# A two-layer encoder trunk on one core: layer-norm sums in one PSUM bank, consecutive dense matmuls on alternating banks, other first transfers and another last output

## The chip, the cores and the metric

The kernel runs on one core of one Trainium2 chip. The metric is the device time of one execution in microseconds (us); of several runs the median is given. A profiled execution also gives a trace: every instruction on the matrix engine (PE, with its weight loads as PEld), the vector engine (DVE), the scalar engine (ACT), GpSimd (POOL) and SyncE (SP), which here only issues transfers, and every DMA transfer. The span of the trace reaches from the first to the last instruction; the profiled execution's own time is a little longer.

## The reference

256 tokens of 2048 numbers pass two layers. Each layer is a mixer, a cross-attention into 256 memory tokens and a gated convolutional FFN, each on an RMS norm of the stream and added to it:

```python
for layer in range(DEPTH):
    h = rms_norm(x, norm_mix_g[layer])
    if layer % 2 == 0:
        # conv branch: GLU, depthwise conv of width 31, LayerNorm, swish; and differential attention
        x = x + mixer_conv_diff(h, ...)
    else:
        x = x + mixer_s5(h, ...)          # state-space scan both ways, GELU, GLU
    x = x + memory_cross_attention(rms_norm(x, norm_xa_g[layer]), rms_norm(mem, norm_mem_g[layer]), ...)
    x = x + conv_ffn(rms_norm(x, norm_ffn_g[layer]), ...)
return rms_norm(x, final_g)
```

Everything is float32. The LayerNorm of the conv branch (`conformer_conv`) is the one whose sums the change touches: mean and variance over 1024 channels, `y = (xf - mu) * lax.rsqrt(var + eps) * g + b`. The last line is the final RMS norm over 2048 numbers of a token.

## The kernel before

**Weights and splitting.** Nearly all the work is dense products of the 256 tokens with weights that come from memory. A weight tile of 128 x 1024 numbers (`raw`, 512 KB, four buffers) is fetched by SP (L204), split by ACT into a rounded high part `hi` (L209) and by DVE into the rest, `lo` (L211); the activations are kept as a high and a low part too. The product is then the sum of three matmuls in a faster format, high by high, low by high and high by low. This is the helper `wtile`, and every dense layer goes through it, 960 times in all.

**Two shapes of product.** `lin_ws` (glu, q and k, memory keys, cross-attention queries, FFN up) holds weights still in the array: a weight block of 128 x 128 against the tokens. For each of 16 input blocks (`kk`) and each of two output blocks (`c`), it issues a short matmul of 256 columns (L253, the weights' low part) and a long one of 512 columns (L250, the weights' high part against both parts of the activations). Output block c accumulates in its own PSUM bank, so the order of banks is 0, 0, 1, 1. One call is 64 matmuls. `lin_xs` (values, output projections, FFN down, the S5's GLU) holds the activations still: for each input block and each half of the tokens (`tb`) three matmuls of 512 columns (L287), with a bank for each half: banks 0, 0, 0, 1, 1, 1.

**Order of the work.** The program is written out by a scheduler with a timing model, which sets the order on each engine. Work beside the dense stream (the depthwise convolution and its LayerNorm `conv_ln`, the S5's parameters) is a Python generator in a list `side`; after each weight tile, `background` lets as much of it into the program as a credit allows. What is left when the memory's keys and values are done is drained, and then the output projection of the first mixer starts with its first half (`bo`, the differential attention's heads) for two output chunks, and its second half (`ao`, the conv branch).

**PSUM buffers.** Besides two `acc` tiles for the dense products there is a pool with two tags, `ps` and `pt`, of two banks each. `pst()` without a tag alternates between the two. The attention heads take two `ps` banks for scores and then `pt` banks for the transposed weights (L457), the output (L463) and its transpose (L476). In `conv_ln` the sums over channels are matmuls with a matrix of ones: `ps_mu` (L518) takes one bank by `pst()`, `ps_var` (L527) the next by another `pst()`.

**First and last.** At the start SP fetches the first quarter of `x`, the identity matrix, gains, the first weight tile and the other quarters in turn with further tiles; POOL fetches five small arrays. At the end the last `lin_xs` keeps the second token half's matmuls of the last three weight tiles for the end (L290, `tail=3`). Then for each half: add to the stream (L694), square and sum (ACT, L696), multiply the last quarter by the final gain (L697; the other quarters had theirs earlier), the reciprocal square root on 128 x 1 numbers (`rsqrt_steps`, L111 to L118: two integer steps and three iterations of four operations), scaling by quarters on ACT (L706) and DVE (L708), and eight output transfers (L709).

## Time and profile before

| | |
|---|---|
| median of 3 runs | 2935.66 us (2931.55 to 2938.13) |
| profiled execution, its own time | 2932.71 us |
| its span | 2930.9 us |
| PE busy, granted clock | 98% of the span, 0.994 |
| DVE, ACT, POOL busy | 76%, 51%, 9% |
| memory traffic | 674 MB, 230 GB/s on average |

A matmul record's end is modelled, and consecutive matmuls overlap in the records: a matmul of 512 columns is recorded with 0.39 us while the next starts 0.23 us after it. So the rate of PE is read from starts, or from the chain of waits, which counts each matmul until the next one starts. The timeline merges neighbours of one line on one engine into one row with a count; the time in brackets is idle time of that engine before the row, and what ended it. Rows named PEld are weight loads and run beside the matmuls.

### The profile page before, as it was taken

How to read it: one execution, taken by the hardware profiler on the slowest of the kernel's cores; microseconds unless marked ns; L12 is line 12 of the kernel's file. 1: busy time of each engine (PE TensorE's matmuls, PEld its weight loads, DVE VectorE, ACT ScalarE, POOL GpSimd, SP SyncE). 2: the span in 40 equal slices, each digit the busy share in tenths (PEclk: the TensorE clock that was granted, in tenths of full speed). 3: DMA queues.
4: the chain of work that ended last, by engine and by line, in shares of the span. 5: the costliest groups of instructions: out<-in, count | busy, mean ns of one | idle time of the engine just before them, and what ended most of it. 6: DMA issues, size and time to landing. Idle time of an engine off the chain costs nothing. (4 is left out here: it accounts for less than half of the span.)

```text
span 2930.9 us, 44468 instructions
## 1 busy us (share of the span) xinstructions
PE 2881.2 (98%) x16769; PEld 2436.5 (83%) x16769; DVE 2213.4 (76%) x3568; ACT 1493.2 (51%) x2015; POOL 268.2 (9%) x509
## 2 busy tenths in 40 slices
PE   8999998999999999999999999999999999999998
PEld 7887887788888888888887787888888888888886
DVE  7899987877899987889855894656567776467764
ACT  5545554554455543455544554545455554345543
POOL 2100022222210012020021121000000000000000
PEclk9999999999999999999999999999999999999999
DMA  6655578988997687776697787655455555555554
GB/s 220 231 188 172 190 238 270 297 260 277 292 297 250 233 272 256 266 254 234 235 316 275 288 328 276 208 187 187 161 191 191 186 188 192 194 189 184 190 188 150
DMA packets 206023, 674.16 MB, mean 230 GB/s; under 512 B 33152, under 2 KB 35728, under 8 KB 205296
## 3 DMA queue, kind: packets, MB, share of 16 engines
q1 hardware_dynamic: 177376, 593.96, 59.1%
q0 software_dynamic: 28432, 77.36, 8.1%
q8 instruction: 131, 2.15, 0.3%
q14 instruction: 84, 0.69, 0.1%
HBM read 620.48 MB, written 61.08 MB: 233 GB/s over the span
## 5 line engine op out<-in xcount | busy, mean ns | idle before, releaser
L211 DVE TENSOR_TENSOR lo<-raw,hi 128x1024 fp32r<-128x1024 f32 x960 | 1173.6, 1224 | 546.1 <-ACT hi L209 542.6
L250 PE MATMUL ps_ws<-x,hi 128*128 128x512 f32 x4352 | 1527.8, 397 | 5.3 <-ACT hi L209 4.4
L209 ACT CAST hi<-raw 128x1024 fp32r<-128x1024 f32 x960 | 1009.0, 1051 | 1005.1 <-PE ps_xs L287 460.8
L253 PE MATMUL ps_ws<-x,lo 128*128 128x256 f32 x4352 | 1202.8, 282 | 2.9 <-DVE lo L211 2.9
L250 PEld LDWEIGHTS ps_ws<-x,hi 128*128 128x128 f32 x4352 | 809.5, 188 | 187.4 <-ACT hi L209 5.2
L253 PEld LDWEIGHTS ps_ws<-x,lo 128*128 128x128 f32 x4352 | 821.6, 189 | 20.0 <-DVE lo L211 5.0
L287 PE MATMUL ps_xs<-hi,hb 128*128 128x512 f32 x1396 | 432.0, 390 | 0.0
L287 PEld LDWEIGHTS ps_xs<-hi,hb 128*128 128x128 f32 x1396 | 262.0, 188 | 53.9
L287 PE MATMUL ps_xs<-lo,hb 128*128 128x512 f32 x698 | 272.3, 390 | 0.0
L287 PE MATMUL ps_xs<-hi,x 128*128 128x512 f32 x640 | 202.8, 395 | 0.2 <-ACT hi L209 0.2
L851 POOL DMA_DIRECT2D w1s<-d_pw x256 | 122.5, 486 | 602.2 <-PE ps_s L438 263.3
L287 PE MATMUL ps_xs<-hi,oT 128*128 128x512 f32 x512 | 160.8, 392 | 0.8 <-ACT hi L209 0.8
L287 PE MATMUL ps_xs<-hi,gT 128*128 128x512 f32 x512 | 159.3, 391 | 0.3 <-ACT hi L209 0.3
L287 PEld LDWEIGHTS ps_xs<-lo,hb 128*128 128x128 f32 x698 | 131.0, 188 | 27.0
L287 PEld LDWEIGHTS ps_xs<-hi,x 128*128 128x128 f32 x640 | 119.9, 189 | 30.3 <-issue 6.1
L287 PE MATMUL ps_xs<-lo,x 128*128 128x512 f32 x320 | 127.3, 398 | 0.0
L259 ACT COPY z<-ps_ws 128x512 f32<-128x512 f32 x88 | 51.7, 587 | 137.6 <-PE ps_ws L250 137.5
L287 PEld LDWEIGHTS ps_xs<-hi,gT 128*128 128x128 f32 x512 | 96.1, 188 | 21.3 <-issue 1.0
L656 ACT ACTIVATE c<-z,fdb,fdw 128x256 f32<-128x256 f32 x176 | 96.2, 595 | 33.0 <-DVE z L651 32.9
L287 PEld LDWEIGHTS ps_xs<-hi,oT 128*128 128x128 f32 x512 | 96.0, 188 | 20.3 <-ACT hi L209 1.0
L512 DVE SCALAR_TENSOR_TENSOR av<-hpt,cdw,av 128x256 f32<-128x256 f32 x240 | 110.7, 485 | 0.7
L260 DVE TENSOR_TENSOR z<-ps_ws,z 128x512 f32<-128x512 f32 x88 | 60.8, 691 | 55.5 <-ACT z L259 55.5
(285 smaller groups left out, 2654.6 us busy)
## 6 DMA issues: line engine op xcount, KB each, us to landing
raw<-ffn_w_up SPq DMA_DIRECT2D x352, 512.0 KB, 3.4
raw<-ffn_w_down SPq DMA_DIRECT2D x176, 512.0 KB, 4.3
raw<-ab_w_in SPq DMA_DIRECT2D x64, 512.0 KB, 3.3
raw<-xa_wv SPq DMA_DIRECT2D x64, 512.0 KB, 3.4
raw<-xa_wk SPq DMA_DIRECT2D x64, 512.0 KB, 4.5
raw<-xa_wq SPq DMA_DIRECT2D x64, 512.0 KB, 4.3
raw<-xa_wo SPq DMA_DIRECT2D x64, 512.0 KB, 3.6
w1s<-d_pw POOLq DMA_DIRECT2D x256, 64.0 KB, 6.1
```

What stands on the lines that cost most here:

```text
L209: nc.scalar.copy(hi, raw)
L211: ins = nc.vector.tensor_tensor(lo, raw, hi.bitcast(F32), op=ALU.subtract)
L250: both = lambda: nc.tensor.matmul(ps[:, c], lhsT=hi[:, kk, sl], rhs=x2, start=first, stop=last)
L253: nc.tensor.matmul(ps[:, c, 1], lhsT=lo[:, kk, sl], rhs=xh, start=False, stop=False)
L259: self.nc.scalar.copy(out, ps[:, :, 1])
L260: self.nc.vector.tensor_tensor(out, ps[:, :, 0], out, op=ALU.add)
L287: ins = mm()
L512: nc.vector.scalar_tensor_tensor(ac[:, ct, :], hp[:, ct, j : j + NTOK], cdw[:, ct, j : j + 1], ac[:, ct, :], op0=ALU.mult, op1=ALU.add)
L656: nc.scalar.activation(c[:, i], zt[:, i, 1 : NTOK + 1], AF.Identity, bias=fdb[:, ft : ft + 1], scale=w(1))
L851: nc.gpsimd.dma_start(pw[t * 16 : t * 16 + 16], self.d_pw[t, k * 4 : k * 4 + 4].partition_broadcast(16))
```

## The change

1. `lin_ws` and `lin_xs` issue the same matmuls in another order. In `lin_ws` the two short ones come one after the other, then the two long ones, so banks alternate 0, 1, 0, 1 (in the first input block the long ones come first). In `lin_xs` the token half is the inner loop.
2. `conv_ln` takes one bank and uses its two halves for the two sums.
3. `rsqrt_steps` multiplies its argument by -0.5 once and joins operations: 9 operations in three iterations in place of 12, and 6 where the tile is one column wide.
4. At the start the identity comes before `x`, the first weight tile is issued from ACT's queue, and the five small arrays come from SP's queue behind the first `lin_ws` in place of POOL's; the small computation of `lam` that needs one of them is written behind the glu stage.
5. At the end the last product's two token halves accumulate in two separate tiles of the pool in place of one `acc` tile; the multiplication by the last quarter's gain is joined with the scaling; quarter 0 and 3 are scaled by DVE, 1 and 2 by ACT.

```diff
@@ setup @@
+        nc.sync.dma_start(self.ident, a["ident"])
         nc.sync.dma_start(self.X[:, :, 0:512], a["x"][0])
-        nc.sync.dma_start(self.ident, a["ident"])
+        self.begun = False
@@ rsqrt_steps @@
+        nc.vector.tensor_scalar(v, v, -0.5, None, op0=ALU.mult)
         for it in range(3):
-            nc.vector.tensor_tensor(t, y, y, op=ALU.mult)
-            nc.vector.tensor_tensor(t, t, v, op=ALU.mult)
-            nc.vector.tensor_scalar(t, t, -0.5, 1.5, op0=ALU.mult, op1=ALU.add)
-            nc.vector.tensor_tensor(out if it == 2 else y, y, t, op=ALU.mult)
+            if v.shape[-1] == 1:
+                nc.vector.scalar_tensor_tensor(t, y, y, v, op0=ALU.mult, op1=ALU.mult)
+            else:
+                nc.vector.tensor_tensor(t, y, y, op=ALU.mult)
+                nc.vector.tensor_tensor(t, t, v, op=ALU.mult)
+            nc.vector.scalar_tensor_tensor(out if it == 2 else y, t, 1.5, y, op0=ALU.add, op1=ALU.mult)
@@ wtile @@
-        dma = nc.sync.dma_start(raw, src)
+        dma = (nc.sync if self.begun else nc.scalar).dma_start(raw, src)
+        self.begun = True
@@ lin_ws @@
-                for c in range(2):
-                    sl = slice(c * 128, c * 128 + 128)
-                    both = lambda: nc.tensor.matmul(ps[:, c], lhsT=hi[:, kk, sl], rhs=x2, start=first, stop=last)
-                    if first:
-                        both()
-                    nc.tensor.matmul(ps[:, c, 1], lhsT=lo[:, kk, sl], rhs=xh, start=False, stop=False)
-                    if not first:
-                        both()
+                sl = [slice(c * 128, c * 128 + 128) for c in range(2)]
+                both = lambda c: nc.tensor.matmul(ps[:, c], lhsT=hi[:, kk, sl[c]], rhs=x2, start=first, stop=last)
+                low = lambda c: nc.tensor.matmul(ps[:, c, 1], lhsT=lo[:, kk, sl[c]], rhs=xh, start=False, stop=False)
+                for part in (both, low) if first else (low, both):
+                    for c in range(2):
+                        part(c)
@@ lin_xs @@
-                for tb in range(2):
-                    sl = slice(tb * 128, tb * 128 + 128)
-                    ops = [(xh, hi, first, False), (xh, lo, False, False), (xl, hi, False, last)]
-                    for x, y, st, sp in ops:
+                for x, y, st, sp in [(xh, hi, first, False), (xh, lo, False, False), (xl, hi, False, last)]:
+                    for tb in range(2):
+                        sl = slice(tb * 128, tb * 128 + 128)
@@ mixer0, behind the first lin_ws @@
+                for t, v in ((cdw, a["conv_dw"]), (cv, a["conv_v"]), (lq, a["diff_l"].partition_broadcast(128)), (nabs, a["nabs"]), (sub_g, a["subln_g"])):
+                    nc.sync.dma_start(t, v)
@@ conv_ln @@
-        pm = self.pst("ps_mu")
+        pm = self.pst("ps_ln")
+        pv = pm[:, NTOK:]
+        pm = pm[:, :NTOK]
...
-        pm = self.pst("ps_var")
         for ct in range(8):
-            nc.tensor.matmul(pm[:, :NTOK], lhsT=self.ones, rhs=sq[:, ct, :], start=ct == 0, stop=ct == 7)
+            nc.tensor.matmul(pv, lhsT=self.ones, rhs=sq[:, ct, :], start=ct == 0, stop=ct == 7)
@@ ffn, the last product @@
-                ps = self.lin_xs(..., tail=3 if last and n == 3 else 0)
+                ps = self.lin_xs(..., ps=[self.pst(f"ps_e{tb}", ("ps", "pt")[tb]) for tb in range(2)] if last and n == 3 else None, start=True, tail=3 if last and n == 3 else 0)
...
-            nc.vector.tensor_tensor(x, x, fg[:, 1536:2048], op=ALU.mult)
...
-                if n % 2:
+                if n == 3:
+                    nc.vector.scalar_tensor_tensor(x, x, r, fg[:, 1536:2048], op0=ALU.mult, op1=ALU.mult)
+                elif n:
                     nc.scalar.activation(x, x, AF.Copy, scale=r)
```

How the order on the engines moves is seen at three places. The first is PE in an FFN-up product of the second layer, within one weight tile; `x2` is the tile of activations, `lo` and `hi` the parts of the weight tile. Before:

```order
L253 MATMUL ps_ws_24100<-x2_20730,lo_24171 128x256
L250 MATMUL ps_ws_24100<-x2_20730,hi_24169 128x512
L253 MATMUL ps_ws_24100<-x2_20730,lo_24171 128x256
L250 MATMUL ps_ws_24100<-x2_20730,hi_24169 128x512
L253 MATMUL ps_ws_24100<-x2_20730,lo_24171 128x256
```

And now, around the end of one product and the start of the next:

```order
L255 MATMUL ps_ws_22684<-x2_20699,lo_22755 128x256 x2
L254 MATMUL ps_ws_22684<-x2_20699,hi_22753 128x512 x2
L254 MATMUL ps_ws_22787<-x2_20189,hi_22790 128x512 x2
L255 MATMUL ps_ws_22787<-x2_20189,lo_22792 128x256 x4
L254 MATMUL ps_ws_22787<-x2_20189,hi_22790 128x512 x2
L255 MATMUL ps_ws_22787<-x2_20189,lo_22792 128x256 x2
```

Short and long matmuls alternated one by one; now they come in pairs, and at a product's start four long and four short ones follow each other.

The second place is PE at the LayerNorm's second sums. `ps_oT` is the transpose of a head's output, `bo` the heads' part of the output projection's input, `sq` the squares. Before:

```order
L287 MATMUL ps_xs_4728<-lo_4762,bo_2510 128x512
L287 MATMUL ps_xs_4728<-hi_4760,bo_2510 128x512
L287 MATMUL ps_xs_4728<-hi_4779,bo_2510 128x512
L476 MATMUL ps_oT_3050<-ident_76,on_3026 128x128 x2
L527 MATMUL ps_var_3960<-sq_3883,ones_81 128x256 x8
L287 MATMUL ps_xs_4728<-lo_4781,bo_2510 128x512
```

And now:

```order
L254 MATMUL ps_ws_4048<-x2_2417,hi_4075 128x512 x2
L527 MATMUL ps_ln_3853<-sq_3863,ones_81 128x256 x8
L255 MATMUL ps_ws_4048<-x2_2440,lo_4100 128x256 x2
L475 MATMUL ps_oT_2898<-ident_76,on_2876 128x128 x2
L456 MATMUL ps_wT_2929<-ident_76,s_2903 128x128 x4
```

The second sums stood behind the last head's transpose, in the middle of the output projection. They now stand in the memory keys' products, ahead of the sixth of eight heads' transpose and 39 dense matmuls behind the first sums.

The third place is DVE at the end: `ps_e0` and `ps_e1` are the last product's two token halves, `fg` the final gains, `fv` and `rsq` the reciprocal square root's small tiles, `fr` its result. Before:

```order
L694 TENSOR_TENSOR X_75<-X_75,ps_xs_26693 128x512 x2
L697 TENSOR_TENSOR X_75<-X_75,fg_26307 128x512
L700 TENSOR_REDUCE fv_26878<-ss_26306 128x1
L697 TENSOR_TENSOR X_75<-X_75,fg_26307 128x512
L700 TENSOR_REDUCE fv_26910<-ss_26306 128x1
L701 TENSOR_SCALAR fv_26878<-fv_26878 128x1
```

And now:

```order
L118 SCALAR_TENSOR_TENSOR rsq_t_26850<-rsq_i_26849,fv_26845 128x1
L122 SCALAR_TENSOR_TENSOR fr_26846<-rsq_t_26850,rsq_i_26849 128x1
L694 TENSOR_TENSOR X_75<-X_75,ps_e1_26661 128x512
L709 TENSOR_SCALAR X_75<-X_75,fr_26846 128x512
L705 SCALAR_TENSOR_TENSOR X_75<-X_75,fr_26846,fg_26274 128x512
L699 TENSOR_REDUCE fv_26871<-ss_26273 128x1
```

Both halves' additions stood first and their small steps alternated; now the first half's chain stands whole ahead of the second half's addition.

More of the change, by code (lines that the diff above doesn't have):

```diff
@@ L261, in add_parts, with lin_xs @@
         return out
-    def lin_xs(self, w, xt, kts, ps=None, stop=True, tail=0):
+    def lin_xs(self, w, xt, kts, ps=None, stop=True, tail=0, start=False):
         nc = self.nc
-        start = ps is None
-        if start:
+        start = start or ps is None
+        if ps is None:
             ps = self.acc.tile([128, 2, 512], F32, tag="acc", name="ps_xs")
@@ L515, in conv_ln @@
         sh = [128, 4, NTOK]
-        pm = self.pst("ps_mu")
+        pm = self.pst("ps_ln")
+        pv = pm[:, NTOK:]
+        pm = pm[:, :NTOK]
         for ct in range(8):
-            nc.tensor.matmul(pm[:, :NTOK], lhsT=self.ones, rhs=ac[:, ct, :], start=ct == 0, stop=ct == 7)
-        nc.vector.tensor_scalar(mu, pm[:, :NTOK], 1.0 / 1024, None, op0=ALU.mult)
+            nc.tensor.matmul(pm, lhsT=self.ones, rhs=ac[:, ct, :], start=ct == 0, stop=ct == 7)
+        nc.vector.tensor_scalar(mu, pm, 1.0 / 1024, None, op0=ALU.mult)
         sq = S.tile([128, 8, NTOK], F32, tag="A0", name="sq")
@@ L672, in ffn @@
                 last = half == 1 and layer == 1
-                ps = self.lin_xs(a[f"ffn_w_down{layer}"][n, k0 : k0 + nk // KD], hv, list(range(nk)), tail=3 if last and n == 3 else 0)
+                ps = self.lin_xs(a[f"ffn_w_down{layer}"][n, k0 : k0 + nk // KD], hv, list(range(nk)), ps=[self.pst(f"ps_e{tb}", ("ps", "pt")[tb]) for tb in range(2)] if last and n == 3 else None, start=True, tail=3 if last and n == 3 else 0)
                 if last and n == 3:
```

23 lines of the change are left out of this document (9 added, 14 removed).

## The prediction

> **What bounds the kernel now.** I read the page first, then the chain of waits, the timeline at the places where PE stands still, and the windows of those stages. PE is recorded busy for 98% of the span, with the two lines of `lin_ws` on top; DVE and ACT have room over the whole.
>
> ```profile
> span 2930.9 us, 44468 instructions
> PE 2881.2 (98%) x16769; PEld 2436.5 (83%) x16769; DVE 2213.4 (76%) x3568; ACT 1493.2 (51%) x2015; POOL 268.2 (9%) x509
> L250 PE MATMUL ps_ws<-x,hi 128*128 128x512 f32 x4352 | 1527.8, 397 | 5.3 <-ACT hi L209 4.4
> L253 PE MATMUL ps_ws<-x,lo 128*128 128x256 f32 x4352 | 1202.8, 282 | 2.9 <-DVE lo L211 2.9
> ```
>
> So the time is the number of matmuls by their rate, and a few stops. The rate stands in the chain of waits (start, length, line, count), where a matmul counts until the next one starts:
>
> ```profile
> 2304.23 0.46 PE ps_ws L250 x2
> 2305.04 0.24 PE ps_ws L253 x2
> 2383.24 0.46 PE ps_ws L250 x2
> ...
> 2451.19 130.56 PE ps_xs L287 x576
> ...
> 2912.20 4.09 PE ps_xs L290 x18
> ```
>
> 576 long matmuls of `lin_xs` take 130.56 us, 226.7 ns each. For `lin_ws`, the row of two long ones marks where one product ends and the next starts; from 2304.23 to 2383.24 seven products pass, 224 pairs of a short and a long one in 79.01 us: 352.7 ns a pair. What short ones cost in a row is seen in the second cross-attention, where 15 of them start between the first and the second of these rows of the timeline (1.80 us, 120.0 ns each):
>
> ```profile
> 2004.12 0.28 PE L574 MATMUL ps_xs<-kT,qT 128*128 128x256 f32 x1
> 2005.92 0.28 PE L253 MATMUL ps_ws<-x,lo 128*128 128x256 f32 x1
> ```
>
> One long and one short one by these rates are 346.7 ns. The alternation in `lin_ws` costs 6.0 ns a pair more.
>
> **The change part by part. Banks in `lin_xs`: nothing.** The 18 late matmuls (L290) all write one bank and take 227.2 ns each; the 576 change the bank at every third one and take 226.7. A same-bank neighbour costs nothing here, and the lines issue the same matmuls, so I put 0.
>
> **Order in `lin_ws`: -10.8 us.** There are 4352 / 2 = 2176 groups of two short and two long ones. At 352.7 ns a pair a group takes 705.4 ns; without any cost of alternation it would be 693.4. The new order changes between lengths once up and once down in a group in place of twice. The rows with x2 show such neighbours as they already stand at a product's edge: two short ones 0.24 us, two long ones 0.46, together 0.70 (rounded to 0.01, so this only says that it lies between the two). I take half the extra as gone, 6.0 ns a group. The bounds: all of it, 12.0 ns; and nothing, since there are stretches in which alternation is free, such as ten pairs between these starts (3.46 us, 346 ns a pair):
>
> ```profile
> 858.12 0.39 PE L250 MATMUL ps_ws<-x,hi 128*128 128x512 f32 x1
> 861.58 0.39 PE L250 MATMUL ps_ws<-x,hi 128*128 128x512 f32 x1
> ```
>
> 2176 groups by 6.0 ns are 13.1 us. Ahead of the first output projection (8 glu, 8 q and k, 8 key products, 24 of 136) DVE is nearly full with the convolution, and I count no gain there:
>
> ```profile
> 200.00:300.00 100.00, 100.00 (x460) 80.77 (x459) 94.92 (x204) 54.59 (x89) 0.00 (x0) 1.00 0.52 178
> ```
>
> (PE, PEld, DVE, ACT, POOL busy, then clock, DMA share and GB/s.) That leaves 112/136 of it, 10.8 us; bounds 0 and 26.
>
> **LayerNorm's bank: -9.6 us.** The largest stop of PE is in the first output projection, for `ao`:
>
> ```profile
> L523 ACT ACTIVATE sq<-av x2: 1056/1059/1062, 403.0 to 404.9; 128x1024 f32<-128x1024 f32 x2
> ...
> 401.26 0.42 DVE L519 TENSOR_SCALAR hpt<-ps_mu 128x256 f32<-128x256 f32 x1
> ...
> 470.87 0.38 PE L476 MATMUL ps_oT<-ident,on 128*128 128x128 f32 x2
> 471.08 3.62 PE L527 MATMUL ps_var<-sq,ones 128*128 128x256 f32 x16
> ...
> 480.93 0.39 PE L287 MATMUL ps_xs<-hi,bo 128*128 128x512 f32 x1
> 491.26 0.79 PE L287 MATMUL ps_xs<-hi,ao 128*128 128x512 f32 x1 [9.94 <-ACT ao L299]
> 494.35 0.39 PE L287 MATMUL ps_xs<-lo,ao 128*128 128x512 f32 x1
> ```
>
> The squares are done at 406, yet their sums start at 471.08, right behind the last head's transposes: the second bank is taken from the buffers that the heads still use. In one bank they follow the squares. From the sums to `ao` took 20.2 us; even if DVE needs twice that between the heads, `ao` is there by 450, 30 us ahead of its use. The stop from 480.93 to 491.26, less one matmul, is 10.1 us. Behind it the clock is half: the seven starts from 491.26 to 494.35 take 3.09 us, at 226.7 ns they would take 1.59. Together 11.6 us. What is late next is the weights:
>
> ```profile
> 440.00:460.00 20.00, 19.95 (x111) 16.81 (x109) 14.99 (x23) 9.09 (x13) 3.81 (x8) 1.00 1.02 324
> 481.00:491.00 10.00, 0.32 (x2) 0.00 (x0) 8.10 (x12) 5.19 (x8) 0.00 (x0) 0.65 0.87 291
> 491.00:510.00 19.00, 18.74 (x81) 15.47 (x82) 13.72 (x17) 9.87 (x16) 3.81 (x8) 0.91 0.49 144
> ...
> ACT hi L209 <- DMA raw<-ab_w_out: 10.0, 6, 3.0
> ```
>
> The transfers are full ahead of the stop and used it to catch up; behind it half is free (0.49 over 19 us, room for the 8.7 us of transfer time that ran in the stop). In this stage (440 to 530) ACT waited 10.0 us for weights, covered so far by four buffers. I take 2 us as showing. Bounds: 0 and 11.6.
>
> **The new wait in it.** PE now meets the second sums 39 dense matmuls, 39 x 0.176 = 6.9 us, behind the first. Mean, subtraction and squares took from 401.3, where DVE reads the first sums, to 406, 4.8 us. Were they later, PE would stand with all dense matmuls behind it, and DVE's `lo` too once its buffers are full; 2 us of room, and I put 0.
>
> **The end: -4.2 us.** After the last matmul the chain of waits and the timeline read:
>
> ```profile
> 2916.32 0.70 DVE X L694
> 2917.04 0.73 ACT junk L696 x2
> 2917.80 0.69 DVE X L697
> 2919.31 0.19 DVE fv L701 x2
> 2921.99 0.08 DVE fr L118
> ...
> 2922.09 2.56 ACT L706 ACTIVATE X<-X,fr 128x512 f32<-128x512 f32 x4 [3.57 <-DVE fr L118]
> 2922.10 1.67 DVE L708 TENSOR_SCALAR X<-X,fr 128x512 f32<-128x512 f32 x4
> 2922.61 4.47 SPq L709 DMA_DIRECT2D out<-X  x8
> ```
>
> Although half 0 is complete at 2912.20, where the 18 late ones begin, its addition waits until 2916.32: the tile is one. In separate tiles half 0 goes: addition 0.70, squares 0.73, then a reduction and ten small steps of about 0.19 each, 2.1 us: `fr` at 2915.8. ACT's two scalings (0.62 each) end at 2917.0, as half 1's addition does. Its squares end at 2917.8; DVE scales half 0 meanwhile (0.42 and, for the joined form, 0.69) until 2918.1; reduction and ten steps to 2920.2; DVE's first quarter at 2920.6, everything scaled at 2921.5. SP needs 0.56 us an issue, so the last of four is out at about 2922.9 in place of 2927.08 (2922.61 + 4.47). What follows, 3.8 us to the end of the span, stays. Bounds: 3 (half 0's chain delays half 1 by a us) and 5.5.
>
> **The start: -2.0 us.**
>
> ```profile
> 10.02 1.04 ACT L209 CAST hi<-raw 128x1024 fp32r<-128x1024 f32 x1 [2.35 <-DMA raw<-ab_w_in]
> 4.50:26.40 21.90, 17.48 (x40) 1.00 0.84 293
> 0.00:10.00 10.00, 1.94 (x8) 1.57 (x8) 0.97 (x2) 3.68 (x7) 6.44 (x18) 1.00 0.74 206
> 10.00:20.00 10.00, 7.91 (x39) 6.83 (x40) 5.68 (x10) 8.69 (x19) 0.00 (x0) 1.00 1.01 396
> ```
>
> The first weights arrive at 10.0; ACT, which splits them and evacuates every transposed `x`, then sets the pace until 26.4 (second row: ACT alone, busy 17.48 of 21.90). Its idle 4.4 us are the upper bound, 0 the lower. The small arrays out of the way, 206 GB/s should come nearer to the later 396, and the first tile in at about 6.5; but ACT's order now has the split first, so that the squares that filled 4.55 to 6.0 wait too. I take 2.0. The Trainium skill (Trainium Kernel Development and Optimization, Key Constraints) says that all queues share the same 16 DMA engines and that another issuing engine saves only issue time; by that, at 206 GB/s, the first tile, `x` and the rest (1.2 MB) would be in at 7.8, and the term -1.
>
> **Small: -0.4 us.** The reciprocal roots lose two of twelve steps; most run beside PE. Ahead of the S5, PE waits 2.3 us for a chain with one of them, two steps of 0.19.
>
> ```profile
> 1563.39 2.82 PE L1024 MATMUL ps_u<-ident,xg 128*128 128x128 f32 x12 [2.31 <-DVE xg L1018]
> ```
>
> Sum: -10.8 - 9.6 - 4.2 - 2.0 - 0.4 = -27.0 us. The profiled execution took 2932.7 us (span 2930.9 and 1.8 around it), so 2905.7. The median shown is 3.0 above that execution: 2908.7, rounded to 2908.
>
> **The rivals.** *The order in `lin_ws` is free* (0.26): the stretch at 858 runs at the summed rate while alternating, so the extra may be a matter of how the stream has locked in, not of the changes. Then 2908 + 10.8 = 2919. [...]
>
> *All of the extra goes* (0.14): 21.6 in place of 10.8 us, 2897. For it: pure rows of either length never show it; against it: one change up and down is left in each group.
>
> *The wait for `ao` becomes one for weights* (0.13): most of the 10.0 us of ACT's waits come to light, 2908 + 8 = 2916. Against: the last 19 us of slack.
>
> *Slower* (0.05): a weight load's record is 188 ns, and two short matmuls in a row leave each next load only 120. If the second short and the first long one waited for their loads, a group would take 2 x 68 ns more, 300 us in all. It decides from 7.4 ns a group on, where the other 16.2 us are used up; beyond 10 ns the kernel is slower. Against: the x2 row of short ones with 0.24, and the 15 in a row.
>
> ```profile
> L287 PEld LDWEIGHTS ps_xs<-hi,hb 128*128 128x128 f32 x1396 | 262.0, 188 | 53.9
> ```
>
> *The change does little of what it says* (0.04): order free and the stop replaced together, 2908 + 10.8 + 9.6 = 2928.
>
> **How the numbers follow.** My forecast, 2908, has 0.38, with 2900 to 2915 as its own range. The range of 8 in 10 reaches to the free order above and to the full gain below: 2894 to 2922. Less than 0.2%, 5.9 us, this kernel's runs can't tell from no change. Forecast, the first three rivals and most of the last are below 2929.8: faster 0.91; same 0.05; slower 0.04.
>
> **What would show it.** In the chain of waits of the changed kernel the distance between two products of the FFN up: 11.29 us now, 11.19 by my forecast, 11.1 with all the extra gone, unchanged if the order is free. The second sums near 408 and no stop at `ao`; a stop for `hi` or `lo` within the output projection would be the third rival. At the end half 0's addition some 4 us ahead of half 1's. Weights' first split at 6 to 7. Wrong would be a `lin_xs` rate other than 226.7, or a group of `lin_ws` above 705 ns.

## The result and the profile after

The changed kernel takes 2915.4 us (median of 4 executions, 2915.1 to 2916.2) against 2934.5 of the kernel before: the ratio is 0.9935, interval 0.9918 to 0.9952. Run once more (five executions, 2910.4 to 2918.7, median 2913.4) the ratio is 0.9936, interval 0.9922 to 0.9949. So it is 19 us faster, and 7 us slower than the forecast of 2908.

The head of the page of the changed kernel, profiled at 2915.3 us:

```profile
span 2913.5 us, 44430 instructions
PE 2869.7 (98%) x16769; PEld 2426.1 (83%) x16769; DVE 2203.7 (76%) x3524; ACT 1492.0 (51%) x2015; POOL 266.0 (9%) x504
```

The span is 17.4 us shorter (2930.9 to 2913.5). To see where, I numbered the 13696 dense matmuls of both traces, which are the same in both kernels, and compared when the same number starts:

| stretch | before | changed | difference |
|---|---|---|---|
| start to matmul 256 | 63.6 us | 59.9 us | -3.7 |
| 256 to 1280 (rest of glu, q and k, values) | 201.5 | 200.7 | -0.8 |
| 1280 to 3072 (heads, LayerNorm, first output projection, queries of the cross-attention) | 431.5 | 432.6 | +1.1 |
| 3072 to the last | 2219.3 | 2209.2 | -10.1 |
| the last one's start to the end | 15.0 | 11.1 | -3.9 |

The third row, "the middle stage" from here on, is where I had expected -9.6.

**The dense order.** The chain of waits of the changed kernel shows four long ones in a row at the edge of two products of the FFN up. Here the first and the last of nine products, and the row of `lin_xs`:

```profile
2238.67 0.93 PE ps_ws L254 x4
...
2339.17 0.93 PE ps_ws L254 x4
...
2440.14 130.57 PE ps_xs L289 x576
```

100.50 us for nine: one product now takes 11.17 us (11.29 before). `lin_xs` with its new order of banks takes 130.57 us for 576 matmuls, where it took 130.56.

That is the second layer, whose 44 FFN-up products take 5.3 us less than before in all. The first layer's 44 gain only 3.0 us, since in the kernel before some of its alternating stretches ran faster. Two starts of short matmuls there, with 27 pairs of a short and a long one between them:

```profile
951.87 0.28 PE L253 MATMUL ps_ws<-x,lo 128*128 128x256 f32 x1
...
961.23 0.27 PE L253 MATMUL ps_ws<-x,lo 128*128 128x256 f32 x1
```

That is 346.7 ns a pair, as much as one short and one long matmul by themselves, and not 352.7. Nine whole products of the kernel before take 11.10 to 11.12 us, less than the 11.17 of the new order; seven of the nine stand right behind a product that was held up (11.9 us or more).

**The LayerNorm.** In PE's timeline of the changed kernel the second sums stand at 396, and the first matmul that reads `ao` comes without a stop:

```profile
396.26 3.62 PE L527 MATMUL ps_ln<-sq,ones 128*128 128x256 f32 x16
...
480.21 0.62 PE L289 MATMUL ps_xs<-hi,ao 128*128 128x512 f32 x2
```

But PE now stands at other places, in the same output projection and in the queries of the cross-attention behind it. Two of them, from the timeline (in brackets the idle time ahead of the row and what ended it):

```profile
503.23 1.04 ACT L301 CAST kT<-kvraw 128x1024 fp32r<-128x1024 f32 x1 [7.17 <-DMA kvraw<-d_kT]
504.18 1.04 ACT L214 CAST hi<-raw 128x1024 fp32r<-128x1024 f32 x1
...
505.27 0.73 PE L289 MATMUL ps_xs<-hi,bo 128*128 128x512 f32 x2 [2.23 <-ACT hi L214]
...
545.56 0.69 DVE L845 TENSOR_TENSOR w1t<-w1s 128x512 f32<-128x512 f32 x1 [4.64 <-DMA w1s<-d_pw]
546.17 1.22 DVE L216 TENSOR_TENSOR lo<-raw,hi 128x1024 fp32r<-128x1024 f32 x1
...
547.45 0.73 PE L289 MATMUL ps_xs<-lo,ao 128*128 128x512 f32 x2 [1.10 <-DVE lo L216]
```

ACT waits 7 us for a tile of the memory's keys, and the weights' split is queued behind it; DVE waits 4.6 us for a piece of the S5's first weights (`w1s`, side work), and the next `lo` is queued behind that. The waits of ACT for weights between 440 and 640, before and then in the changed kernel (us in total, times, longest):

```profile
ACT hi L209 <- DMA raw<-xa_wq: 23.9, 11, 5.2
ACT hi L209 <- DMA raw<-ab_w_out: 12.7, 8, 3.0
```

```profile
ACT hi L214 <- DMA raw<-ab_w_out: 32.7, 19, 6.3
ACT hi L214 <- DMA raw<-xa_wq: 30.8, 12, 4.3
```

And the window 440 to 600 as one row, before and then changed (PE, PEld, DVE, ACT, POOL busy; clock; share of the DMA engines; GB/s):

```profile
440.00:600.00 160.00, 145.16 (x699) 120.29 (x698) 130.40 (x206) 78.10 (x113) 38.23 (x80) 0.95 0.88 284
```

```profile
440.00:600.00 160.00, 151.91 (x749) 124.14 (x747) 124.54 (x187) 73.02 (x101) 42.13 (x88) 0.99 0.93 294
```

PE gets 50 more records into the window, the transfers' share goes from 0.88 to 0.93. PE's own waits between 300 and 640, the largest rows before and then in the changed kernel:

```profile
PE ps_xs L287 <- ACT ao L299: 9.9, 1, 9.9
PE ps_xs L287 <- DVE lo L211: 3.6, 5, 1.5
```

```profile
PE ps_xs L289 <- DVE lo L216: 4.5, 8, 1.1
PE ps_ws L255 <- DVE lo L216: 4.1, 5, 1.6
PE ps_xs L289 <- ACT hi L214: 3.5, 4, 2.2
```

With the smaller rows they add up to 15.0 us before and 14.9 in the changed kernel. The stop at `ao` went, and its 10 us are spread over some twenty smaller ones, nearly all for `hi` and `lo`. (In the second profile of the changed kernel they add up to 10.3.)

**Start and end.** Timeline of the changed kernel: the first split is at 4.73 (10.02 before; forecast at 6 to 7), and at the end the first half's addition is 4.08 us ahead of the second's:

```profile
4.73 1.04 ACT L214 CAST hi<-raw 128x1024 fp32r<-128x1024 f32 x1 [2.27 <-DMA raw<-ab_w_in]
...
2898.79 0.69 DVE L694 TENSOR_TENSOR X<-X,ps_e 128x512 f32<-128x512 f32 x1 [1.77 <-PE ps_e L289]
2902.25 0.16 DVE L122 SCALAR_TENSOR_TENSOR fr<-rsq_t,rsq_i 128x1 f32<-128x1 f32 x1
2902.87 0.69 DVE L694 TENSOR_TENSOR X<-X,ps_e 128x512 f32<-128x512 f32 x1 [0.46 <-PE ps_e L292]
```

### The profile page after: what moved, and what is told of

Its sections match the earlier page's. It is cut to its first block, busy times and chain, and to the rows that moved or that the text cites. A ratio compares the mean times of both kernels' runs of the same rounds, so it can differ in the third digit from the quotient of the medians.

```text
span 2913.5 us, 44430 instructions
## 1 busy us (share of the span) xinstructions
PE 2869.7 (98%) x16769; PEld 2426.1 (83%) x16769; DVE 2203.7 (76%) x3524; ACT 1492.0 (51%) x2015; POOL 266.0 (9%) x504
## 5 line engine op out<-in xcount | busy, mean ns | idle before, releaser
L254 PE MATMUL ps_ws<-x,hi 128*128 128x512 f32 x4352 | 1351.4, 396 | 2.8 <-DVE x L168 1.2
L255 PEld LDWEIGHTS ps_ws<-x,lo 128*128 128x128 f32 x4352 | 793.6, 188 | 186.6 <-DVE lo L216 10.5
L255 PE MATMUL ps_ws<-x,lo 128*128 128x256 f32 x4352 | 844.7, 280 | 6.7 <-DVE lo L216 6.6
L254 PEld LDWEIGHTS ps_ws<-x,hi 128*128 128x128 f32 x4352 | 674.5, 189 | 17.3 <-ACT hi L214 2.5
L289 PE MATMUL ps_xs<-hi,hb 128*128 128x512 f32 x1328 | 357.6, 390 | 0.0
L289 PE MATMUL ps_xs<-lo,hb 128*128 128x512 f32 x664 | 204.9, 390 | 0.0
L289 PE MATMUL ps_xs<-hi,x 128*128 128x512 f32 x640 | 177.5, 394 | 1.5 <-ACT hi L214 1.5
L289 PE MATMUL ps_xs<-hi,oT 128*128 128x512 f32 x512 | 141.1, 392 | 0.8 <-ACT hi L214 0.8
L289 PE MATMUL ps_xs<-hi,gT 128*128 128x512 f32 x512 | 138.2, 391 | 0.3 <-ACT hi L214 0.3
L289 PE MATMUL ps_xs<-lo,x 128*128 128x512 f32 x320 | 100.9, 394 | 0.0
```

Source lines behind the costliest of these rows:

```text
L254: both = lambda c: nc.tensor.matmul(ps[:, c], lhsT=hi[:, kk, sl[c]], rhs=x2, start=first, stop=last)
L255: low = lambda c: nc.tensor.matmul(ps[:, c, 1], lhsT=lo[:, kk, sl[c]], rhs=xh, start=False, stop=False)
L289: ins = mm()
```

## The experiments

The question is the middle stage. Theory one: its limit is the transfers (weights, keys and values, and the S5's first weights, `s5_w1`, which run beside it as side work). Theory two: its limit is DVE, which does that side work's arithmetic and also every `lo`. The expectations call them the weights' or transfer theory and the vector-engine theory. All runs in one table; the stage is that of the profiled execution, whose own time stands in the last column and need not be near the median.

| kernel | median us | ratio to before, interval | middle stage us | profiled us |
|---|---|---|---|---|
| before | 2933.7 to 2934.6 | | 431.5 | 2932.7 |
| changed | 2915.4 | 0.9935, 0.9918 to 0.9952 | 432.6 | 2915.3 |
| changed, again | 2913.4 | 0.9936, 0.9922 to 0.9949 | 429.3 | 2913.4 |
| before with one bank for the LayerNorm | 2930.7 | 0.9990, 0.9981 to 0.9998 | 433.4 | 2935.8 |
| changed with two banks | 2908.6 | 0.9915, 0.9902 to 0.9928 | 427.7 | 2915.4 |
| changed, side work off in the output projection | 2920.4 | 0.9957, 0.9940 to 0.9974 | 417.7 | 2914.6 |
| the same with two banks | 2923.0 | 0.9960, 0.9948 to 0.9972 | 416.2 | 2923.0 |
| changed without 5 of 6 operations of `s5_w1` | 2908.0 | 0.9914, 0.9900 to 0.9927 | 424.7 | 2907.0 |
| changed without 30 of 32 loads of `s5_w1` | 2898.4 | 0.9878, 0.9865 to 0.9892 | 414.9 | 2898.3 |
| changed, side work spread | 2908.7 | 0.9917, 0.9903 to 0.9931 | 417.6 | 2907.9 |
| changed, grouped lengths on the same bank | 2916.7 | 0.9942, 0.9927 to 0.9957 | 430.8 | 2918.9 |
| changed, runs of eight | 2905.7 | 0.9904, 0.9887 to 0.9920 | 424.7 | 2902.9 |
| changed, side work spread otherwise | 2905.5 | 0.9902, 0.9887 to 0.9917 | 418.2 | 2906.3 |
| runs of eight and spread | 2904.4 | 0.9898, 0.9882 to 0.9915 | 422.9 | 2901.7 |

### The LayerNorm's bank alone

Edit of the kernel before:

```diff
-        pm = self.pst("ps_mu")
+        pm = self.pst("ps_ln")
+        pv = pm[:, NTOK:]
+        pm = pm[:, :NTOK]
...
-        pm = self.pst("ps_var")
```

> The kernel before with the LayerNorm's two sums in one bank and nothing else changed. I look at the total and at the stage from the 1280th to the 3072nd dense matmul, which took 431.5 us in the kernel before (265.1 to 696.6) and 432.6 in the changed one (260.6 to 693.2). My forecast: the stop of 10.1 us at `ao` and its half clock go, the stage takes 422 and the total is 9.6 us lower (ratio 0.9967). The weights' theory (the transfers are what ends last between 440 and 600, and the stop was the time in which they caught up): the stop goes, stops for `hi` and `lo` of the same sum come, the stage stays at 430 to 433 and the ratio is 0.9995 to 1.0005. A vector-engine theory (its side work ends last) gives the same total here.

Measured: 0.9990, interval 0.9981 to 0.9998, so 0.6 to 5.6 us faster, about 3 by the medians. The stage of the profiled execution is 433.4, at the edge of what the weights' theory gave, and the ratio is below it; my 0.9967 is outside the interval. Its profile shows what the theory said: no stop at `ao`, but the waits for the output projection's weights grow from 12.7 to 32.9 us. That profile is the slowest of its eleven executions, 5 us above the median, so 433.4 says less than the ratio.

```profile
482.60 0.39 PE L287 MATMUL ps_xs<-hi,ao 128*128 128x512 f32 x1
```

```profile
ACT hi L209 <- DMA raw<-ab_w_out: 32.9, 17, 5.3
ACT hi L209 <- DMA raw<-xa_wq: 28.6, 12, 7.1
```

### Two banks in the changed kernel

Edit of the changed kernel:

```diff
-        pm = self.pst("ps_ln")
-        pv = pm[:, NTOK:]
-        pm = pm[:, :NTOK]
+        pm = self.pst("ps_mu")[:, :NTOK]
...
+        pv = self.pst("ps_var")[:, :NTOK]
```

> The changed kernel with two banks for the LayerNorm's sums again; all else of the change stays. My forecast: 9.6 us slower than the changed kernel, 2925. The weights' theory: the stop at `ao` comes back and the stops for `hi` and `lo` shrink by as much; within 2 us of the changed kernel, 2913 to 2917, the stage from the 1280th to the 3072nd dense matmul at 431 to 434 us.

Measured: 2908.6, 0.9915; the interval overlaps that of the changed kernel (0.9922 to 0.9949 beside the later kernels), but no run says that one bank is worth anything in the changed kernel. (The profile is the one execution of five at 2915.4.) And I was wrong about the stop: it does not come back.

```profile
444.71 0.38 PE L475 MATMUL ps_oT<-ident,on 128*128 128x128 f32 x2
444.92 1.24 PE L526 MATMUL ps_var<-sq,ones 128*128 128x256 f32 x5
...
475.82 0.61 PE L289 MATMUL ps_xs<-hi,ao 128*128 128x512 f32 x2
```

The second sums still follow the last head's transposes, but that head now stands behind 2080 dense matmuls, where it stood behind 2179 before. With two banks the rest of the change brought the last head forward by 99 matmuls; the sums are at 444.9, 31 us ahead of the first use of `ao`, and the way from them to `ao` took 20.2 us before. Which part of the change moved the head I did not separate. The changed kernel itself does not have the head there: with one bank it stands behind 2168, at 470.9, and sums that waited for it would, with the same 20.2 us, give `ao` at 491 (an estimate), 11 us behind its first use at 480.2. So the stop went in two different ways, in one kernel by the bank and in the other by the head's place, and the time stays.

### Side work off in the output projection, with one bank and with two

Edit of the changed kernel; the second kernel has the two banks of above as well. `RATE` is what `background` gives to the side work for each weight tile.

```diff
-RATE = {"glu": 1.2, "qkv": 1.29, "kv": 0.95, "out": 0.8, "wq": .7, "wo": .8, "up": .75, "down": 0.96}
+RATE = {"glu": 1.2, "qkv": 1.29, "kv": 0.95, "out": 0.0, "wq": .7, "wo": .8, "up": .75, "down": 0.96}
```

> The changed kernel with the side work's rate at 0 in the first output projection (the S5's first weights, each piece 1.5 MB of transfers and 6 vector operations of 0.68 us, are not run beside its 32 weight tiles; some 17 of 32 pieces come later). Weights' or vector-engine theory: with about 6 pieces, 9 MB, out of the 100 us of that stage, the stops for `hi` and `lo` there (10 of the 14 us between 487 and 640) mostly go: the stage from the 1280th to the 3072nd dense matmul 423 to 427 in place of 432.6, the total 2906 to 2910 unless the work that comes later stops PE in the FFN. If neither, 432 and 2915.

> The same rate of 0, but with two banks for the LayerNorm's sums. If the bank's gain was hidden by the side work, then here, where that is gone, two banks cost their price: the stop of 10 us at `ao` is there and nothing is regained, so 8 to 11 us slower than the same kernel with one bank. If the bank is worth nothing whatever the side work does: within 2 us of it.

Measured: the stage falls to 417.7 and 416.2, lower than I had put it. The window row (440 to 600) of the first of the two: PE is busy nearly throughout, the transfers' share is 0.78 in place of 0.93.

```profile
440.00:600.00 160.00, 159.16 (x827) 134.40 (x826) 111.63 (x162) 82.46 (x115) 19.06 (x40) 1.00 0.78 247
```

But the total does not fall: 2920.4 and 2923.0. What was put off comes back: in the first kernel matmuls 3072 to 7168 take 824.6 us in place of the changed kernel's 818.8, and 7168 to 8192 take 280.5 in place of 271.9, 14.4 us more in all. The arithmetic on the S5's second weights, which is side work too, ends some 70 us later (1490 in place of 1421), and I take it that its transfers then run beside other weights, those of the second memory values. ACT's waits for these weights between 1500 and 1680, in this kernel and in the changed one:

```profile
ACT hi L214 <- DMA raw<-xa_wv: 18.3, 8, 5.2
```

```profile
ACT hi L214 <- DMA raw<-xa_wv: 9.3, 4, 3.2
```

As for the banks: I had expected the second kernel 8 to 11 us slower, by a stop that it does not have. It is 2.6 slower by the medians with overlapping intervals, and its stage is not longer. This run says nothing on the price of a stop, only that no gain of the bank is to be seen here either; the first kernel's executions reach from 2914.6 to 2929.9, and its profile is the fastest of them.

### Operations or loads

Edit of the changed kernel, the first in each of the 32 pieces:

```diff
-            tt(t, pw[:, :, 1], b[:, :, 1], MUL)
...
-            tt(b[:, :, 0], b[:, :, 0], t, SUB)
+            tt(b[:, :, 0], b[:, :, 0], pw[:, :, 0], SUB)
```

> The changed kernel without five of the six vector operations of each of the 32 pieces of the S5's first weights (left out: the complex product that forms them, so the S5's weights are not the reference's); their transfers and their places in the program stay. Some 15 pieces lie between 400 and 640, so 15 x 5 x 0.68 = 51 us of DVE are gone there. Vector-engine theory: the stage from the 1280th to the 3072nd dense matmul falls from 432.6 to 417 to 423, as in the kernel whose side work is put off (417.7). Transfer theory: the transfers are the same, it stays at 428 to 434.

And the second:

```diff
-            if k < 31:
+            if k < 1:
                 load(k + 1)
```

> The changed kernel in which 30 of the 32 pieces of the S5's first weights are not fetched (left out: their 1 MB of loads, of which 512 KB from GpSimd's queue; the vector operations run on the first two pieces' buffers, so the S5's weights are not the reference's); operations and stores stay. Some 15 MB of 65 MB are gone between 400 and 640. Transfer theory: the stage from the 1280th to the 3072nd dense matmul falls from 432.6 to 417 to 424. Vector-engine theory: it stays at 428 to 434.

Measured: 424.7 without the operations, 414.9 without the loads (2908.0 and 2898.4 in total). The window rows 440 to 600, first without the operations:

```profile
440.00:600.00 160.00, 152.32 (x749) 124.70 (x749) 96.21 (x126) 77.33 (x104) 41.95 (x88) 0.99 0.95 303
```

then without the loads, with two rows of its waits:

```profile
440.00:600.00 160.00, 158.66 (x823) 134.64 (x823) 137.30 (x205) 81.72 (x115) 0.00 (x0) 1.00 0.72 239
```

```profile
ACT hi L214 <- DMA raw<-xa_wq: 20.0, 13, 4.3
ACT hi L214 <- DMA raw<-ab_w_out: 2.6, 3, 1.4
```

DVE loses 28 of its 124.5 us and PE issues as many matmuls in the window as in the changed kernel (749; 684 dense ones in place of 672, and the second profile of the changed kernel has 762 and 686); the transfers' share rises to 0.95. With the loads gone, PE issues 823, although DVE is busier than ever (137.3), and the waits for the output projection's weights fall from 32.7 to 2.6 us. So between 440 and 600 the transfers are the limit, and DVE is not. Nor do the loads cost only because DVE stands in its order for a late piece, as at 545: without the operations DVE waits for no piece between 440 and 640 (9.6 us in the changed kernel), and still ACT's waits for the weights of the output projection and the queries are 57.4 us there, against 63.5 in the changed kernel and 22.6 without the loads. But 424.7 lies between the two theories' ranges, so one of the two alone does not tell it all: outside of that window less work on DVE seems to help. From 600 to 640, without the operations and then in the changed kernel:

```profile
600.00:640.00 40.00, 38.73 (x243) 33.93 (x242) 25.94 (x33) 20.36 (x27) 10.18 (x22) 1.00 0.82 253
```

```profile
600.00:640.00 40.00, 35.37 (x214) 29.94 (x213) 29.60 (x42) 20.89 (x32) 7.68 (x16) 1.00 0.77 241
```

So DVE seems to have a share of the stage, the smaller one; these are single profiles, and the second one of the changed kernel has 225 matmuls there.

What the transfers were in the window 440 to 600: without the loads, and in the changed kernel, there with its rows by queue (packets, MB, share of 16 engines):

```profile
DMA packets 11190, 38.20 MB, mean 239 GB/s; under 512 B 1194, under 2 KB 1194, under 8 KB 11178
```

```profile
DMA packets 14734, 47.07 MB, mean 294 GB/s; under 512 B 2693, under 2 KB 2693, under 8 KB 14722
...
q1 hardware_dynamic: 11901, 41.15, 77.7%
q0 software_dynamic: 2821, 5.78, 14.7%
```

8.9 MB less in the window, though more weights pass in it. Two thirds of that, 5.78 MB, are GpSimd's queue, and the output projection's weights, which come by SP's, then hardly wait; those of the queries still do (20.0 us). What the loads by SP's queue and those by GpSimd's cost each was not separated. The Trainium skill (Trainium Kernel Development and Optimization, Key Constraints) says that the queues share the same 16 DMA engines; the trace agrees, by the 2.6 us above.

### Spreading the side work

Edits of the changed kernel, the first kernel's and then the second one's:

```diff
-RATE = {"glu": 1.2, "qkv": 1.29, "kv": 0.95, "out": 0.8, "wq": .7, "wo": .8, "up": .75, "down": 0.96}
+RATE = {"glu": 1.2, "qkv": 1.29, "kv": 0.95, "out": 0.3, "wq": .7, "wo": .9, "up": .75, "down": 1.12}
```

```diff
-RATE = {"glu": 1.2, "qkv": 1.29, "kv": 0.95, "out": 0.8, "wq": .7, "wo": .8, "up": .75, "down": 0.96}
+RATE = {"glu": 1.2, "qkv": 1.29, "kv": 0.95, "out": 0.3, "wq": .7, "wo": .7, "up": .75, "down": 1.2}
```

> The changed kernel with the side work's rate at 0.3 in place of 0.8 in the first output projection, and 0.9 in place of 0.8 and 1.12 in place of 0.96 in the cross-attention's output projection and the FFN down, so that what is put off is made up before the S5. With the rate at 0 the stage from the 1280th to the 3072nd dense matmul fell by 15 us, but 14 came back between the 6144th and the 8192nd, where the side work then ended 75 us later. Either theory: here the stage is at 421 to 427, and the later stages give back at most 3: 2906 to 2911. If the gain comes back whole whatever the spread: 2915.

> The changed kernel with side rates 0.3 in the first output projection, 0.7 in the cross-attention's output projection (0.9 in the kernel spread before, which stood still for 5 us at 765 to 772, at the FFN's start) and 1.2 in the FFN down (1.12 there). The stage from the 1280th to the 3072nd dense matmul again 417 to 421; between the 3328th and the 3712th no more than 50 us (49.3 in the changed kernel, 54.4 in the kernel spread before); total 2902 to 2906. If the 5 us come back elsewhere: 2908.

Measured: 2908.7 and 2905.5; the stage is 417.6 and 418.2. The first gave 6.7 us back at the FFN's start, more than I allowed, in several short stops of which this is the longest at that place:

```profile
769.52 0.47 PE L255 MATMUL ps_ws<-x,lo 128*128 128x256 f32 x2 [0.88 <-DVE lo L216]
```

The second has none of it: from matmul 3328 to 3712 it takes 71.6 us, as the changed kernel does, and the first 78.4 (the figures 49.3 and 54.4 in the expectation are those to matmul 3584; the number in it was wrong). From 3712 to 7168, over the FFN, it gives back 7.5. Its total lies in the range expected, 8 to 10 us under the changed kernel; each was compared with the kernel before, 0.9902 and 0.9936, and the intervals (0.9887 to 0.9917 and 0.9922 to 0.9949) do not overlap.

### The changed kernel again

> The changed kernel itself, once more, beside the kernels that leave work out. With two banks it had 2908.6 in most executions and 2915.4 in the profiled one, while the changed kernel's four executions lie between 2915.1 and 2916.2. If one bank is dearer than two here, these are again at 2915 to 2916; if the two kernels are alike and only executions differ, they spread between 2908 and 2916.

Measured: 2910.4 to 2918.7, median 2913.4. The executions spread, as the second case says; 2908.6 of the two-bank kernel is below all of them, so whether one bank is the dearer one stays open.

### Banks or lengths

Edits of the changed kernel; first the order short 0, short 1, long 1, long 0:

```diff
-                for part in (both, low) if first else (low, both):
-                    for c in range(2):
+                for part, cs in ((both, (0, 1)), (low, (1, 0))) if first else ((low, (0, 1)), (both, (1, 0))):
+                    for c in cs:
```

> The changed kernel with the order short 0, short 1, long 1, long 0 in a group of `lin_ws`: lengths stay grouped (two changes of length in a group of four), but half of the neighbours write the same bank, as in the kernel before. If it is the lengths that cost: the FFN-up product stays at 11.17 us (before 11.29) and the total at that of the changed kernel, 2913 to 2915. If it is the banks: 11.23 to 11.29, and 5 to 10 us slower.

Then runs of eight:

```diff
-            for kk in range(4):
-                xh, _, x2 = xt(k4 * 4 + kk)
...
+            for kind in ("long", "short") if k4 % 2 == 0 else ("short", "long"):
+                for kk in range(4):
+                    xh, _, x2 = xt(k4 * 4 + kk)
+                    for c in range(2):
+                        sl = slice(c * 128, c * 128 + 128)
+                        if kind == "long":
+                            nc.tensor.matmul(ps[:, c], lhsT=hi[:, kk, sl], rhs=x2, start=k4 + kk == 0, stop=k4 + kk == 6)
+                        else:
+                            nc.tensor.matmul(ps[:, c, 1], lhsT=lo[:, kk, sl], rhs=xh, start=False, stop=False)
```

> The changed kernel with eight long and eight short matmuls of a weight tile in turn (long, short, short, long, long, ... from tile to tile: 4 changes of length in a product of 64 matmuls in place of 32; banks still alternate). If the cost is by change of length: the changed kernel has 11.17 us a product against 11.09 by the single rates, so with an eighth of the changes 11.10, and 136 x 0.07 = 9 us off the total where PE sets the pace, 2904 to 2908. If what is left has another cause: 11.17 and 2913 to 2915. Slower if a whole tile's `lo` is needed too early or too late: stops for `lo` in every product.

Measured: 2916.7 and 2905.7. Edges of products in the chain of waits, first with half of the neighbours on the same bank, four products apart:

```profile
2253.42 0.93 PE ps_ws L254 x4
...
2298.09 0.93 PE ps_ws L254 x4
```

then with runs of eight (sixteen where two runs meet):

```profile
2231.73 3.65 PE ps_ws L256 x16
2235.39 1.91 PE ps_ws L258 x16
...
2242.87 3.65 PE ps_ws L256 x16
```

On the same bank a product takes 11.17 us (44.67 for four), as on alternating ones: once the lengths are grouped the banks cost nothing, and the gain is that of grouping. But a change of length has no fixed price. The 27 pairs of the kernel before at 951.87, and its nine products at 11.10 to 11.12 us, have the alternating order and are faster than any `lin_ws` product of the changed kernel. What puts a stretch into the slower rhythm was not found. The total, 2916.7, is 1.7 over what I gave for this case; its intervals overlap with those of the changed kernel. In runs of sixteen a product is 11.14 us (2242.87 - 2231.73), a group of four 696 ns. In the second layer, where nearly every FFN-up product took 11.29 us before, the step from 64 to 32 changes of length gave 0.12 us, that from 32 to 4 another 0.03, less than the 0.07 I had expected. The long ones are then at 228.1 ns, the short ones at 119.4, so two of each make 695. The Trainium skill (TensorE: Matmul & The Clock Gate, Back-to-back issue gap) gives N/2.4 + 2.5 ns for an isolated matmul at the full clock, by which, as an estimate, they would take 215.8 and 109.2 ns. For a stream of weight loads and matmuls, which this is, it says that both set the spacing and gives about 131 ns for 512 columns; no row here is as low as either, and the rows decide.

Only a part of the 8 to 10 us that runs of eight gain in total is this rate: by it they gain 0.5 us for 16 products, and from matmul 3072 to the last one they gain 4.6 in all. The rest is in the middle stage of the profiled execution, 424.7; why the order of matmuls eases it was not tested.

### Runs of eight and spread side work together

Edit of the kernel with runs of eight:

```diff
-RATE = {"glu": 1.2, "qkv": 1.29, "kv": 0.95, "out": 0.8, "wq": .7, "wo": .8, "up": .75, "down": 0.96}
+RATE = {"glu": 1.2, "qkv": 1.29, "kv": 0.95, "out": 0.3, "wq": .7, "wo": .7, "up": .75, "down": 1.15}
```

> The changed kernel with both findings: runs of eight in `lin_ws` (2905.7 by itself) and the side rates 0.3 in the first output projection, 0.7 in the cross-attention's output projection, 1.15 in the FFN down (2905.5 by itself, with 1.2). The gain of the rates lies in the stage from the 1280th to the 3072nd dense matmul, where the runs of eight had gained some of the same (424.7 in place of 432.6); what the runs gain outside of it is 0.5 us for 16 products, some 4 us over the FFN and the cross-attention. If the two add where they don't overlap: 2899 to 2903; if not, 2905.

Measured: 2904.4, 0.9898, interval 0.9882 to 0.9915. The two gains do not add: each alone has 2905.5 to 2905.7. It is the fastest kernel that leaves nothing out, below the changed kernel's interval (0.9922 to 0.9949, the later of its two) and 30 us below the kernel before, but not told apart from its two parts.

## Why the prediction was right and wrong

The 2915.4 lies inside 2894 to 2922, 7 above the forecast, and by the size of its miss it is the third rival's figure, 2916. Term by term, in the profiled executions:

| term | forecast | measured |
|---|---|---|
| order in `lin_ws` | -10.8 | -10.1 behind matmul 3072, some of the -0.8 ahead of 1280; within the middle stage not separated |
| LayerNorm's bank | -9.6 | +1.1 (the second profile: -2.2; alone in the kernel before: -3 by the medians) |
| end | -4.2 | -3.9 |
| start | -2.0 | -3.7 |
| banks in `lin_xs` | 0 | 0 (130.57 for 130.56) |
| small | -0.4 | not seen: PE's wait ahead of the S5 is 2.62 us, 2.31 before |

**The step that failed** is "what is late next is the weights ... I take 2 us as showing". The mechanism was named and its size was not: of the 11.6 some 9 came back in the kernel before (about 3 us were gained there by the bank alone), and in the changed kernel's two profiles the stage is between 1.1 us longer and 2.2 shorter. I took the 19 us of slack behind the stop, where the transfers' share is 0.49, for room that stays. I now read that share as low because tiles had arrived during the stop (8.7 us of transfer time ran in it); this is argued, not measured. With no stop, PE asks for the same bytes earlier, and between 440 and 600 the engines were at 0.88 already. The run without the loads shows that the transfers set this stage: 1 MB less a piece, and it falls by 14 to 18 us, with nothing changed at the LayerNorm. A warning could have been read before: 160 us at a share of 0.88 leave 19 us of transfer time in all, and if the weights arrive behind the side work's transfers, which is argued too, not all of it can be used.

**A premise that holds in part.** I put the late second sums down to the second bank alone. With two banks and the rest of the change the sums are in time as well, 26 us earlier, because the last head stands 99 matmuls earlier there. In the changed kernel it stands only 11 earlier, so there the one bank is what brings the sums forward. Neither the diff nor the order of the changed kernel's instructions shows what two banks would do.

**What held.** The stop at `ao` is gone, the second sums came without a stop of their own, and a stop for `hi` and `lo` in the output projection was given as the sign of the third rival: it is there, at 505 and 547. The FFN-up product was forecast at 11.19 and is 11.17 in the second layer: 7.5 ns a group, not 6.0. It is the grouping of lengths that gains; that banks have no part was argued in the prediction from `lin_xs` alone and is shown by the same-bank order. From 64 to 32 changes about three quarters of what is to be had went there, not half. The rival with slower weight loads is out: steady products are at 698 ns a group, and sixteen short ones in a row take 119.4 ns each.

**Luck in the order's term.** That -10.1 lies so near -10.8 is in part luck. The gain of a steady product was larger than forecast (0.12 us, and not 0.10), and fewer products gained it: the 104 products behind matmul 3072 would have made 12.5 us by the steady gain (an estimate), but the first layer's 44 gave 3.0 and not 5.3. So the ground of the rival in which the order is free, that the extra is a matter of how the stream has locked in and not of the changes, holds for a part of the kernel before; as a forecast of the time it is out.

**The start** gained 1.7 more than forecast: the first matmul is only 0.7 us earlier, but from there ACT has hardly any gap. Its window in the changed kernel, from the first split to the last evacuation of `x`:

```profile
4.50:23.00 18.50, 14.97 (x81) 13.09 (x82) 14.79 (x52) 17.02 (x40) 0.26 (x1) 1.00 0.95 349
```

1.5 us idle in place of 4.4, so two thirds of the bound and not half; the stretch is 3.4 us shorter. The first tile was in at 4.7, ahead of the 6.5 and of the 7.8 that were worked out. **The end** is as worked out, but for 0.3.

The terms sum to -17.4 where -27.0 was forecast, a miss of 9.6. I had added 3.0 us because the median of the kernel before stood that much above its profiled execution; the changed kernel's median is that of its profile, so these 3.0 hid a part of the miss. One sum is off in the chances: forecast, three rivals and most of the last one add up to about 0.94, where "faster" was given 0.91.

## What to carry to other kernels

A stop at a late operand, in a stretch where the DMA engines are near 0.9 as here, can also be the time in which the transfers catch up; before counting it as a gain, work out the bytes of the whole stretch against its length without the stop, the side work's bytes among them. Moving side work out of such a stretch paid here only when it was put off in part: put off whole, the total was 2920; put off in part and made up in the FFN down, 2905.5. Where matmuls of two lengths alternate, compare their spacing with that of each length by itself in several stretches; where it is larger, grouping by length took most of the difference away here, and which bank they write did not matter.

## What the runs showed that was not expected

- In steady products three quarters of the cost of alternating lengths goes with the first halving of the changes: 705, 698 and 696 ns a group with 64, 32 and 4 changes of length in a product, and the two shapes' own rates (228 and 119 ns in runs of sixteen) sum to 695. But the same alternating order also ran without any such cost, at 693 ns for two of each (27 pairs at 346.7 ns), in the first layer of the kernel before.
- In a stretch limited by transfers, 28 us less work on DVE did not let PE issue more matmuls in 160 us (749, for 749 and 762 in two profiles of the changed kernel), while 9 MB less in transfers (47.1 to 38.2 MB) let it issue 823.
- A kernel's executions spread by as much as the effects here: the two-bank kernel had 2908.5 to 2909.8 four times and 2915.4 once, and the kernel with side work off 2914.6 to 2929.9. Of such a kernel one profile is one case; that the order in which the transfers land makes the spread was not tested.
